# A short-convolution mixer on one core: u tiles that begin inside a 64-byte line of SBUF

## The chip, the core and the metric

The kernel runs on one NeuronCore of a Trainium2 chip. A core has a matrix engine (TensorE, PE in the profile; its weight loads are listed as PEld), three elementwise engines (VectorE or DVE, ScalarE or ACT, GpSimd or POOL) and a queue engine (SyncE or SP) that issues most transfers. They share SBUF, a memory of 128 partitions, and meet through semaphores. The time is microseconds on the device for one execution. Before: median 773.86 us of 3 runs (773.32 to 774.14).

## What is computed

One layer of an encoder trunk on x of 1024 frames by 1024 channels, fp32: a norm, four projections of 2048 channels each, a causal convolution of three taps, two gates, a projection back, a second norm and the residual.

```python
def short_conv_mixer(u, w_in, conv_w, w_out):
    z, bg, cg, v = jnp.split(u @ w_in.astype(u.dtype), 4, axis=-1)
    y = bg * causal_dwconv(cg * v, conv_w) * jax.nn.silu(z)
    return y @ w_out.astype(u.dtype)

u = rms_norm(h, pre_norm[i])
m = short_conv_mixer(u, sc_w_in[j], sc_conv_w[j], sc_w_out[j])
h = h + rms_norm(m, post_norm[i])
```

## The kernel before

**Products.** Every fp32 operand is split into a high part and a low part of type fp32r, and each product is three matmuls: low by high, high by low, high by high. The 2x2 block product of a projection is done with seven block products (a, b, c, d, e, f, g) instead of eight, after Strassen and Winograd, and three of these (b, f, g) are split into seven smaller ones once more for most column blocks. The operand of the moving side is a **u tile**, `u_a` to `u_g`: 2 parts x 4 k-blocks x 512 columns of fp32r, 16,384 bytes in each partition. The stationary side is a weight block of 128 x 128 out of a **page** of 2,048 bytes, which VectorE and ScalarE split as it comes in from HBM. So a block product is 12 matmuls of 512 columns, all reading one u tile; each writes one PSUM bank.

```python
nc.tensor.matmul(ps, lo, UH[i][:, k], start=first and k == 0, stop=False, skip_group_check=True)
nc.tensor.matmul(ps, hi, UL[i][:, k], start=False, stop=False, skip_group_check=True)
nc.tensor.matmul(ps, hi, UH[i][:, k], start=False, stop=last, skip_group_check=True)
```

The first argument after the bank is the stationary operand, the second the moving one. The profile names a matmul by bank, moving tile and stationary tile: `px<-u_d,wdh` moves `u_d` over the high part of weight block d.

**The smaller products** of b, f and g move 256 columns. Some of them move halves of `u_b`, `u_f` and `u_g`; the others move sums that were built once and are kept in tiles of their own, named `ubch_deep`, `ubgl_deep` and so on, in a pool (`tmp`) behind the pages.

**The stages.** A head (to about 40 us) loads x, norms and transposes it and builds the u tiles; then 32 pairs of weight columns (two for each of 16 channel blocks) run through the products, while VectorE adds results out of PSUM, runs the convolution and splits the next weights; from about 610 us the output projection runs, with both sides split into tiles of the same pool as the u tiles: `ou_a` to `ou_g` move, `oy_a` to `oy_g` are stationary; for the smaller products `oA..`, `oB..` and `ox..`. All of these are called u tiles here, since they are made with the tag `u`.

**Order.** The kernel is recorded first and then arranged by a planner (`Plan`), which simulates the engines with costs of its own and writes out one fixed order for each engine. It knows sizes and uses, not addresses.

**Memory.** In each partition SBUF holds, from the bottom: a scratch and small constants, the pool `up` with seven buffers for u tiles, 32 pages, and `tmp`. All buffers of `up` and all pages begin on a multiple of 64 bytes. The first tile of `tmp` is `gpad`, 1,026 floats, 4,104 bytes, which is rounded to 4,128; the `deep` tiles are stacked behind it and so begin 32 bytes into a 64-byte line.

**Lines.** The class `Tile` (from line 161) makes the real tile in `get`; every operation is issued from line 252, a helper, so the profile gives all of them as L252 and they are told apart by their tiles. The tiles with the tag `u` are made in `new_u` (line 802), for the second half of x (`xb`, line 989), in `third_unit` (1540), `split_pages` (1553) and `split_small` (1609).

Of the kernel before, what the change touches and what calls it, by code (L numbers as in the profile page):

```python
# [157 lines left out]
        return out  # L158


class Tile(View):

    __slots__ = ("pool", "args", "kw", "made", "parts", "writes", "reads", "left", "space", "key", "read", "summed", "n", "slot")
# [11 lines left out]
    def get(self):  # L175
        if self.made is None:
            kw = self.kw
            if kw["tag"] == "pg":
                kw = dict(kw, tag=f"pg{self.slot}", bufs=1)
            self.made = self.pool.pool.tile(list(self.args[0]), self.args[1], **kw)  # L180
        return self.made


# [1882 lines left out]
```

## Time and profile before

| | |
|---|---|
| median of 3 runs | 773.86 us (773.32 to 774.14) |
| the profiled execution | 772.83 us |
| its span, first to last instruction | 771.0 us |
| mean granted TensorE clock | 0.998 |
| HBM read, written | 101.74 MB, 44.30 MB |
| span, mean rate | 189 GB/s |

The busy time of an engine is what the profile calls busy: instructions in flight, without queue work. Matmuls overlap: one is issued while the one before it is still draining, so a group's mean (`390`) is the time that one takes from its own start to its own end, longer than the distance to the next one's start. In a row of the timeline the first figure is the start in us from the start of the span, the second the duration of the row's instructions together, and `x63` says that 63 of them were merged. A row of the waits reads: who waited, for whom, total us, times, longest.

### The profile page before, as it was taken

What the parts mean: (1) busy time and instruction counts of PE and PEld (TensorE: products, weight loads), DVE (VectorE), ACT (ScalarE), POOL (GpSimd) and SP (SyncE); (2) the same over time, 40 slices, a digit from 0 to 9 for tenths busy, and PEclk for the clock granted to TensorE, in tenths of its full rate; (3) what the DMA queues carried; (4) which work ended last, traced back from release to release, by engine and by line L of the source; (5) the groups of instructions that cost most, each with busy time, mean ns of one, the idle gap of its engine ahead of it and who ended that gap; (6) DMA issues with size and microseconds to landing.
All of it is one profiled execution on the core that took longest, in us unless ns stands there. A gap on an engine that the chain in (4) does not pass through costs nothing.

```text
span 771.0 us, 12816 instructions
## 1 busy us (share of the span) xinstructions
PE 762.2 (99%) x4320; PEld 669.6 (87%) x4320; DVE 673.9 (87%) x1022; ACT 458.8 (60%) x880; POOL 462.2 (60%) x416
## 2 busy tenths in 40 slices
PE   8999999999999999999999999999999999999996
PEld 7888889898889898888888898988888889889885
DVE  6899988989988978989999989798999898877993
ACT  7765678575656565556556565556653656564831
POOL 2519997889575778696789777584739100600321
PEclk9999999999999999999999999999999999999999
DMA  9222325243333547576858474927465998666842
GB/s 318 66 56 82 119 85 152 101 126 131 97 116 96 171 111 209 126 191 158 239 137 254 116 215 107 249 84 213 122 180 174 335 367 293 197 218 206 274 150 109
DMA packets 117137, 130.11 MB, mean 169 GB/s; under 512 B 7320, under 2 KB 74704, under 8 KB 116944
## 3 DMA queue, kind: packets, MB, share of 16 engines
q1 hardware_dynamic: 112560, 120.77, 49.0%
q0 software_dynamic: 4352, 8.39, 7.1%
q8 instruction: 34, 0.56, 0.3%
q14 instruction: 31, 0.25, 0.1%
q10 hardware_dynamic: 160, 0.14, 0.0%
HBM read 101.74 MB, written 44.30 MB: 189 GB/s over the span
## 4 chain that ended last, share of the span: by engine, by line
PE 98%; DVE 1%; DMA 0%; ACT 0%; POOL 0%; issue 0%; POOLq 0%; ACTq 0%
PE px L252 39%; PE pv L252 15%; PE po_x L252 11%; PE px2b L252 5%; PE px2f L252 4%; PE px2g L252 3%; PE po_v L252 3%; PE pp L252 3%; PE pv2b L252 3%; PE pv2f L252 2%; PE pf_x L252 1%; PE pb_x L252 1%; PE py2b L252 1%; PE pv2g L252 1%; PE py L252 1%; PE pf_v L252 1%
## 5 line engine op out<-in xcount | busy, mean ns | idle before, releaser
L252 PE MATMUL px<-u_d,wdh 128*128 128x512 f32 x248 | 76.8, 390 | 0.0
L252 PE MATMUL px<-u_a,wah 128*128 128x512 f32 x248 | 76.7, 390 | 0.0
L252 PE MATMUL pv<-u_e,weh 128*128 128x512 f32 x248 | 76.7, 390 | 0.0
L252 PE MATMUL px<-u_c,wch 128*128 128x512 f32 x248 | 76.6, 390 | 0.0
L252 ACT COPY beside<-raw 128x512 f32<-128x512 f32 x67 | 39.6, 591 | 31.8 <-DVE wal L252 11.0
L252 PEld LDWEIGHTS px<-u_d,wdh 128*128 128x128 f32 x248 | 46.6, 188 | 9.1
L252 PEld LDWEIGHTS px<-u_c,wch 128*128 128x128 f32 x248 | 46.7, 188 | 9.0
L252 PEld LDWEIGHTS px<-u_a,wah 128*128 128x128 f32 x248 | 46.7, 188 | 8.9
L252 PEld LDWEIGHTS pv<-u_e,weh 128*128 128x128 f32 x248 | 46.6, 188 | 8.9
L252 DVE SCALAR_TENSOR_TENSOR cv<-gpad,cw,cv 128x1024 f32<-128x1024 f32 x32 | 49.7, 1554 | 3.4 <-ACT cv L252 3.3
L252 POOL TENSOR_TENSOR sf<-raw,sc 128x512 f32<-128x512 f32 x30 | 44.5, 1482 | 10.9 <-DVE sc L252 6.0
L252 PE MATMUL px<-u_d,wdl 128*128 128x512 f32 x124 | 48.7, 393 | 0.0
L252 PE MATMUL px<-u_a,wal 128*128 128x512 f32 x124 | 48.7, 393 | 0.0
L252 PE MATMUL px<-u_c,wcl 128*128 128x512 f32 x124 | 48.5, 392 | 0.0
L252 PE MATMUL pv<-u_e,wel 128*128 128x512 f32 x124 | 48.5, 391 | 0.0
L252 POOL TENSOR_TENSOR sc<-se,raw 128x512 f32<-128x512 f32 x25 | 36.5, 1460 | 19.0 <-DVE se L252 10.0
L252 ACT COPY sna<-px 128x512 f32<-128x512 f32 x30 | 17.6, 586 | 49.4 <-PE px L252 47.7
L252 POOL TENSOR_TENSOR raw<-raw,raw 128x512 f32<-128x512 f32 x31 | 44.8, 1446 | 3.3 <-DVE se L252 1.9
L252 POOL TENSOR_TENSOR rs_post<-ve_post,minus_half 128x1 f32<-128x1 f32 x7 | 5.4, 784 | 68.1 <-DVE ve_post L252 68.1
L252 POOL TENSOR_TENSOR se<-raw,raw 128x512 f32<-128x512 f32 x22 | 33.1, 1504 | 17.7 <-DMA raw<-in_sc_w_in 5.7
L252 DVE TENSOR_TENSOR wcl<-sc,wch 128x512 fp32r<-128x512 f32 x31 | 31.6, 1020 | 2.6 <-ACT wch L252 2.6
L252 DVE TENSOR_TENSOR sna<-px2b,sna 128x256 f32<-128x256 f32 x56 | 23.2, 413 | 11.9 <-PE px2b L252 11.9
(486 smaller groups left out, 2637.1 us busy)
## 6 DMA issues: line engine op xcount, KB each, us to landing
raw<-in_sc_w_in SPq DMA_DIRECT2D x128, 256.0 KB, 4.6
y_d<-cv SPq DMA_DIRECT2D x16, 512.0 KB, 3.1
s_d<-s SPq DMA_DIRECT2D x32, 256.0 KB, 4.8
t_d<-in_sc_w_out POOLq DMA_DIRECT2D x16, 512.0 KB, 8.2
tb<-in_sc_w_out SPq DMA_DIRECT2D x16, 256.0 KB, 3.0
t_d<-in_sc_w_out SPq DMA_DIRECT2D x16, 256.0 KB, 4.5
t_d<-t_d SPq DMA_DIRECT2D x16, 256.0 KB, 4.5
s<-y_d SPq DMA_DIRECT2D x16, 256.0 KB, 4.7
```

The source lines that it names most:

```text
L252: getattr(engine, name)(*(self.plain(a) for a in args), **{k: self.plain(a) for k, a in kw.items()})
```

## The change

A u tile is asked for with 64 bytes more than it needs, as a flat row, and the tile that is used is a view of that row which begins some floats in: 8, 4, 12 or 2 floats, so 32, 16, 48 or 8 bytes. Which of them is taken from a table by the first letter of the last part of the tile's name: `u_a` and `ou_a1` have `a`, `oA1_b` and `ox_b` have `b`. `xb`, the second half of x, stays at 0. The planner's costs, the order on all engines and the waits are the same as before; so are the sizes of all operands. The buffers of `up` lie 16,448 instead of 16,384 bytes apart, and everything behind them begins 448 bytes later.

```diff
+EDGES = {"x": 0, "a": 8, "c": 4, "d": 12, "e": 2, "b": 4, "f": 8, "g": 12, "A": 4, "B": 8}
...
-            self.made = self.pool.pool.tile(list(self.args[0]), self.args[1], **kw)
+            shape = list(self.args[0])
+            if kw["tag"] == "u":
+                at, whole = EDGES[kw["name"].split("_")[-1][0]], int(np.prod(shape[1:]))
+                t = self.pool.pool.tile([shape[0], whole + 16], self.args[1], **kw)[:, at : at + whole]
+                names = "abcd"[: len(shape) - 1]
+                sizes = dict(zip(names[1:], shape[2:]))
+                self.made = t.rearrange(f"p ({' '.join(names)}) -> p {' '.join(names)}", **sizes)
+            else:
+                self.made = self.pool.pool.tile(shape, self.args[1], **kw)
         return self.made
```

| bytes into the line | tiles |
|---|---|
| 8 | `u_e`, `ou_e`, `oy_e` |
| 16 | `u_b`, `u_c`, `ou_c`, `oy_c`, `oA.._b`, `oB.._b`, `ox_b` |
| 32 | `u_a`, `u_f`, `ou_a`, `oy_a`, `oA.._f`, `oB.._f`, `ox_f` |
| 48 | `u_d`, `u_g`, `ou_d`, `oy_d`, `ou_g`, `oy_g` |

## The prediction

> **What bounds the kernel now.** I read the page first: which engine is full, and which the chain of waits runs through.
>
> ```profile
> span 771.0 us, 12816 instructions
> PE 762.2 (99%) x4320; PEld 669.6 (87%) x4320; DVE 673.9 (87%) x1022; ACT 458.8 (60%) x880; POOL 462.2 (60%) x416
> ...
> PE 98%; DVE 1%; DMA 0%; ACT 0%; POOL 0%; issue 0%; POOLq 0%; ACTq 0%
> ```
>
> PE holds 98% of the chain. A busy PE may still be a waiting PE, so the waits of PE alone came next:
>
> ```profile
> PE pw L252 <- DVE idle L252: 1.1, 1, 1.1
> PE pp L252 <- ACT u_a L252: 0.5, 1, 0.5
> PE pk L252 <- DVE xa L252: 0.3, 1, 0.3
> ```
>
> Three waits, 1.9 us, all on the way to the first products. From then on PE runs matmul after matmul, and the time is the number of matmuls times the distance between two starts. Only what changes that distance counts. The means in the groups (389 ns) are latencies of overlapping instructions and do not give it; the timeline does.
>
> ```profile
> L252 PE MATMUL po_x<-ou_g,oy_g 128*128 128x512 f32 x96 | 21.9, 389 | 0.0
> ...
> 749.81 14.44 PE L252 MATMUL po_x<-ou_g,oy_g 128*128 128x512 f32 x63
> ```
>
> 63 matmuls of 512 columns end 14.44 us after the first start, the last of them 0.389 us long: (14.44 - 0.39) / 62 = 226.6 ns from start to start. Now the 256-column ones, in one stretch where two kinds stand side by side:
>
> ```profile
> 127.29 0.28 PE L252 MATMUL px2b<-ubgh_deep,dwb 128*128 128x256 f32 x1
> ...
> 127.99 0.28 PE L252 MATMUL pv<-ufgh_deep,dwf 128*128 128x256 f32 x1
> ...
> 128.69 0.28 PE L252 MATMUL px<-u_g,dwg0l 128*128 128x256 f32 x1
> ...
> 129.41 0.28 PE L252 MATMUL px2g<-u_g,dwg0l 128*128 128x256 f32 x1
> ...
> 130.13 0.40 PE L252 MATMUL px<-u_a,wal 128*128 128x512 f32 x1
> ```
>
> Twelve matmuls that move a `deep` tile take 128.69 - 127.29 = 1.40 us, 116.7 ns each; twelve that move u_g take 130.13 - 128.69 = 1.44 us, 120.0 ns each. Same columns, same kind of weights, no wait in either. In the layout the u tiles begin on a 64-byte line and the `deep` tiles 32 bytes into one (they are stacked behind gpad, 4,104 bytes long). So the trace of before already holds the experiment, at one offset: 32 bytes are 3.3 ns faster than 0.
>
> From 512 to 256 columns the distance falls by 226.6 - 120.0 = 106.6 ns, 0.416 ns a column. What is left at 0 columns, 120.0 - 106.6 = 13.4 ns, is a fixed charge per matmul: 32 columns' worth at offset 0, and 24 columns' worth (10.1 ns) at offset 32. The 8 columns saved are 32 bytes of fp32: just what the first line no longer holds.
>
> **The change part by part.** No instruction is added, removed or moved on any engine, and the semaphores waited for are the same. What moves are addresses. (1) The moving operand of every matmul on a u tile starts 8, 16, 32 or 48 bytes into a line; so does the stationary one in the output products. (2) A u tile is 64 bytes longer, so u buffers spread by 64 bytes each and all pages behind shift by 448 bytes, whole lines. The `deep` tiles keep their 32 bytes.
>
> How many matmuls get which offset is counted from the groups; three of them for d and three for g, and three for e:
>
> ```profile
> L252 PE MATMUL px<-u_d,wdh 128*128 128x512 f32 x248 | 76.8, 390 | 0.0
> L252 PE MATMUL px<-u_d,wdl 128*128 128x512 f32 x124 | 48.7, 393 | 0.0
> L252 PE MATMUL po_x<-ou_d,oy_d 128*128 128x512 f32 x96 | 21.9, 389 | 0.0
> L252 PE MATMUL px<-u_g,wgh 128*128 128x512 f32 x56 | 17.3, 390 | 0.0
> L252 PE MATMUL px<-u_g,wgl 128*128 128x512 f32 x28 | 10.9, 390 | 0.0
> ...
> L252 PE MATMUL pv<-u_e,weh 128*128 128x512 f32 x248 | 76.7, 390 | 0.0
> L252 PE MATMUL pv<-u_e,wel 128*128 128x512 f32 x124 | 48.5, 391 | 0.0
> L252 PE MATMUL po_v<-ou_e,oy_e 128*128 128x512 f32 x96 | 21.9, 389 | 0.0
> ```
>
> With 512 columns: at 48 bytes d 248 + 124 + 96 and g 56 + 28 + 96 = 648; at 8 bytes e 468 and 24 in the first products = 492; at 32 bytes a 492 (as e) and f 84 = 576; at 16 bytes c 468 (as d) and b 60 = 528. With 256 columns: b 504 at 16, f 480 at 32, g 288 at 48. Together 3,516.
>
> Only 32 bytes have a price in the trace. For 8, 16 and 48 I bound it by the rows next to them. Floor: they change nothing, as at 0; then only 576 + 480 = 1,056 matmuls save 3.33 ns, 3.5 us. Ceiling: what counts is not the first line but the last, which 8 bytes of offset leave nearly empty; then the shortest offsets save most (5.8 ns at 8, 5.0 at 16, 3.3 at 32, 1.7 at 48, which is the same line read from the other end) and the sum is 2.9 + 5.2 + 3.5 + 1.6 = 13.1 us. Below nothing, too: see the slower rival. I take the straight line through the two points that are measured, 0.104 ns a byte, because it says what the 8 saved columns say: 0.83, 1.67, 3.33 and 5.00 ns. The sum: 492 x 0.83 = 0.4 us, 1,032 x 1.67 = 1.7, 1,056 x 3.33 = 3.5, 936 x 5.00 = 4.7; **10.3 us** of the 752 us in which PE runs products, 1.4%.
>
> Where would a faster PE meet a limit? First the head, where VectorE builds the u tiles just in time:
>
> ```profile
> 42.59 2.35 DVE L252 TENSOR_TENSOR u_c<-xb,u_c 128x1024 fp32r<-128x1024 f32 x2
> ...
> 48.34 2.35 DVE L252 TENSOR_TENSOR u_d<-xa,u_d 128x1024 fp32r<-128x1024 f32 x2
> ...
> 45.15 0.39 PE L252 MATMUL px<-u_c,wcl 128*128 128x512 f32 x1
> ...
> 50.59 0.39 PE L252 MATMUL px<-u_d,wdl 128*128 128x512 f32 x1
> ```
>
> u_c is done at 44.94 and used at 45.15; u_d is still being written when its first half is used. What PE gains before 50.6 us, 38 x 1.4% = 0.5 us, it waits away again. Then the middle and the DMA stretch:
>
> ```profile
> 550.00:600.00 50.00, 50.00 (x267) 43.23 (x266) 46.64 (x66) 24.73 (x45) 33.49 (x27) 1.00 0.57 175
> 600.00:650.00 50.00, 50.00 (x282) 43.98 (x282) 45.60 (x81) 29.08 (x53) 2.93 (x2) 1.00 0.95 328
> ```
>
> In its fullest late window VectorE (46.64, the third figure with a count) still idles 3.4 us of 50, five times the 0.7 us by which PE shortens it, so it keeps up. The DMA engines are 95% busy from 600 to 650 us (0.95, last but one); I count the 0.7 us of that stretch as lost. The closest handover in between:
>
> ```profile
> 419.01 0.68 DVE L252 TENSOR_TENSOR wdl<-beside,wdh 128x512 fp32r<-128x512 f32 x1
> ...
> 419.89 0.40 PE L252 MATMUL px<-u_d,wdl 128*128 128x512 f32 x1
> ...
> DVE sna L252 <- PE px2b L252: 11.9, 14, 1.6
> ```
>
> 0.20 us early. But VectorE has no lead of its own to lose: it waits for PE in turn (one such wait 14 times, about once in each of the 37 us rounds), so it moves forward with PE, and of the 6 us gained until then at most one round's 0.5 us can meet this margin. That is 0.3 us at the one or two tightest places; I charge nothing and leave it to the range. That VectorE and ScalarE now write u tiles off the line I cost at nothing: a `deep` tile, 32 bytes off, is written as fast as a page that stands on a line,
>
> ```profile
> 98.14 0.69 DVE L252 TENSOR_TENSOR dwf0l<-beside,dwf0h 128x512 fp32r<-128x512 f32 x1 [0.93 <-ACT beside L252]
> ...
> 99.68 0.69 DVE L252 TENSOR_TENSOR ubcl_deep<-beside,ubch_deep 128x512 fp32r<-128x512 f32 x1 [0.34 <-ACT beside L252]
> ```
>
> and there are some 300 such writes in 700 us.
>
> Gain: 10.3 - 0.5 - 0.7 = 9.1 us. The profiled execution took 772.83 us (its span of 771.0 and 1.8 around it), 1.0 under the median of 773.86. Against it the sum gives 763.7, against the median **764.8 us**.
>
> **Rivals.** *Only whole halves of a line help* (0.16): 32 and 48 bytes save 3.33 ns, 8 and 16 nothing: 1,056 + 936 = 1,992 matmuls, 6.6 us, less 0.9 in the two stretches: 768.2. For it: 32 is the only offset seen.
>
> *The last line decides* (0.10): the ceiling above, 13.1 - 1.2: 762.0. For it: the `deep` rows cannot tell first from last, since 32 bytes leave 8 columns in both.
>
> *The offset is not the cause* (0.07): the `deep` tiles also lie elsewhere in SBUF, behind the pages. Then 773.9, or a little more if a start inside a 16-byte piece makes one more piece to fetch: 4 columns at 0.416 ns, 1.7 ns on the 492 matmuls at 8 bytes, 0.8 us, 774.7. Against it: u tiles lie from 3 to 118 KB and all show 120.0 or 226.6. The Trainium skill's "SBUF — State Buffer", section "Specifications (TRN2)", speaks for this rival: it gives SBUF lines of 16 bytes with a penalty for each crossing to a new one, so that 16, 32 and 48 should be as good as 0 and 8 slightly worse. The rows above disagree: 32 bytes, two such lines on, read 116.7 ns against 120.0.
>
> *Slower* (0.13): a start that is not on 32 bytes costs one more half line per matmul, 8 columns, because the row of 512 or 256 columns then begins and ends in a piece of a half. That is 528 + 492 + 648 + 504 + 288 = 2,460 matmuls at 8, 16 and 48 bytes; at +3.33 ns each 8.2 us, against 3.5 us saved at 32 bytes: +4.7 us, 778.6. It decides from 3.5 / 2,460 = 1.4 ns a matmul. Against it, on another engine:
>
> ```profile
> L252 DVE SCALAR_TENSOR_TENSOR cv<-gpad,cw,cv x32: 1268/1334/2317, 67.8 to 612.0; 128x1024 f32<-128x1024 f32 x32
> ```
>
> half of these read gpad from byte 4 of a line and half from byte 8. VectorE's 512 columns above took 0.69 us, so 1,024 columns in 1,268 ns leave no room for anything read twice. For PE nothing shows it either way.
>
> Inside the forecast (0.54) there is a smaller fork: if the distance between moving and stationary operand counts, not the line, then the output products, where both move alike, gain nothing: 2.4 us of the 10.3, 767.2.
>
> **How the numbers follow.** Faster by over 0.2% (1.5 us, about what this kernel's measurement can tell from no change): forecast, halves, last line, 0.54 + 0.16 + 0.10 = 0.80. Within: 0.07. Slower: 0.13. The range runs from 760.5, below the last-line case by the spread of the runs, to 772.0, where only the 32-byte tiles pay (773.9 - 3.5 + 1.2 = 771.6); no change and slower, 0.20, stay out.
>
> **What would show it.** Blocks of twelve 512-column matmuls in the late timeline, start to start: 225.8 ns for e, 224.9 for c, 223.3 for a, 221.6 for d and g; 256-column blocks of b 118.3, f 116.7, g 115.0. All of PE's waits together should grow by no more than 1.2 us. If e is the quickest, the last line rules; if c and e stay at 226.6, the halves; if c, d and e rise above 226.6, the slower rival; if a and f do not fall, the offset was never the cause. The forecast is also wrong if the distances fall as said and the span does not: then a wait that PE did not have before takes it.

## The result

| | before | after |
|---|---|---|
| median of the runs | 773.86 us (773.32 to 774.21) | 780.96 us (780.76 to 781.33) |
| ratio of the medians | | 1.0093 (95% interval 1.008 to 1.0107) |
| the profiled execution | 772.83 us | 780.93 us |
| its span | 771.0 us | 779.2 us |
| mean granted TensorE clock | 0.998 | 0.998 |

The change makes the kernel slower by 0.93%, where 1.2% faster was predicted; the time lies outside the range. The first view of the page of the changed kernel, the engines' busy time and the shares of the chain:

```profile
span 779.2 us, 12816 instructions
...
PE 770.4 (99%) x4320; PEld 668.0 (86%) x4320; DVE 673.3 (86%) x1022; ACT 458.9 (59%) x880; POOL 462.1 (59%) x416
...
PE 98%; DVE 0%; DMA 0%; ACT 0%; POOL 0%; issue 0%; POOLq 0%; ACTq 0%
```

The span has grown by 8.2 us and PE's busy time by the same 8.2 us (762.2 to 770.4). No other engine has more to do: VectorE went from 673.9 to 673.3 us, ScalarE from 458.8 to 458.9. PE's waits in the changed kernel (who waited, for whom, total us, times, longest):

```profile
PE pw L263 <- DVE idle L263: 1.1, 1, 1.1
PE pp L263 <- ACT u_a L263: 0.5, 1, 0.5
PE pk L263 <- DVE xa L263: 0.4, 1, 0.4
```

They are the same three, 2.0 us instead of 1.9. So nothing waits longer, and the loss lies in the distance between the starts of two matmuls. First the stretch that the prediction read, in the timeline after the change (start, duration):

```profile
129.81 0.28 PE L263 MATMUL px2b<-ubgh_deep,dwb 128*128 128x256 f32 x1
...
131.21 0.28 PE L263 MATMUL px<-u_g,dwg0l 128*128 128x256 f32 x1
...
132.62 0.39 PE L263 MATMUL px<-u_a,wal 128*128 128x512 f32 x1
...
135.42 0.28 PE L263 MATMUL px<-u_g,dwg2l 128*128 128x256 f32 x1
```

Twelve matmuls that move a `deep` tile take 131.21 - 129.81 = 1.40 us as before. Twelve of 256 columns that move u_g take 1.41 us, 117.5 ns each, a gain of 2.5 ns (5.0 was predicted). The twelve of 512 columns behind them, on u_a, take 135.42 - 132.62 = 2.80 us, 233.3 ns each, where 223.3 was predicted. The same block of u_e, at the same place of the program, before the change:

```profile
102.27 0.39 PE L252 MATMUL pv<-u_e,wel 128*128 128x512 f32 x1
...
104.99 0.28 PE L252 MATMUL px2b<-u_b,dwb0l 128*128 128x256 f32 x1
```

and after it:

```profile
104.60 0.39 PE L263 MATMUL pv<-u_e,wel 128*128 128x512 f32 x1
...
107.39 0.28 PE L263 MATMUL px2b<-u_b,dwb0l 128*128 128x256 f32 x1
```

2.72 us became 2.79: 226.7 ns, then 232.5. And the output projection, in long unbroken rows, before:

```profile
720.54 21.95 PE L252 MATMUL po_x<-ou_d,oy_d 128*128 128x512 f32 x96
742.33 21.92 PE L252 MATMUL po_x<-ou_g,oy_g 128*128 128x512 f32 x96
```

and after:

```profile
689.81 18.39 PE L263 MATMUL po_v<-ou_e,oy_e 128*128 128x512 f32 x76
...
727.97 22.26 PE L263 MATMUL po_x<-ou_d,oy_d 128*128 128x512 f32 x96
750.07 22.40 PE L263 MATMUL po_x<-ou_g,oy_g 128*128 128x512 f32 x96
```

From the start of ou_d to that of ou_g, 96 matmuls, it was 21.79 us (227.0 ns) and is 22.10 (230.2). For ou_e, 8 bytes into its line, (18.39 - 0.40) / 75 = 239.9 ns, the longest of all.

Over the whole kernel, interval times count for every u and `deep` tile, from the starts of the records in the two traces: the 2,243 matmuls of 512 columns take 513.0 us before and 523.4 after, the 1,974 of 256 columns 234.5 and 231.9. The sum is +10.4 - 2.5 = +7.9 us of the span's 8.2. So the short matmuls gained, as predicted though by less, and the long ones lost instead of gaining.

### The profile page after: what moved, and what is told of

It reads as the page before. It is cut to its first block, busy times and chain, and to the rows that moved or that the text cites. A ratio compares the mean times of both kernels' runs of the same rounds, so it can differ in the third digit from the quotient of the medians.

```text
span 779.2 us, 12816 instructions
## 1 busy us (share of the span) xinstructions
PE 770.4 (99%) x4320; PEld 668.0 (86%) x4320; DVE 673.3 (86%) x1022; ACT 458.9 (59%) x880; POOL 462.1 (59%) x416
## 4 chain that ended last, share of the span: by engine, by line
PE 98%; DMA 0%; DVE 0%; ACT 0%; POOL 0%; issue 0%; POOLq 0%; ACTq 0%
PE px L263 39%; PE pv L263 15%; PE po_x L263 11%; PE px2b L263 5%; PE px2f L263 4%; PE px2g L263 3%; PE po_v L263 3%; PE pp L263 3%; PE pv2b L263 3%; PE pv2f L263 2%; PE pf_x L263 1%; PE pb_x L263 1%; PE py2b L263 1%; PE pv2g L263 1%; PE py L263 1%; PE pf_v L263 1%
```

## The experiments

The change does two things to addresses. It puts tiles into their lines, and by the 64 bytes that it adds to each buffer it spreads the seven buffers (buffer i moves by 64 i) and moves the pages by 448. **Distance** below is the start of the moving row less that of the stationary row, modulo 256 bytes, from the layout of each kernel. Before, it is 0 for every u tile, over the pages and in the output products, and 32 for the `deep` tiles. The expectations weigh two kinds of reading: that a tile's own start in its line counts (L, later O), and that it is where the two rows lie to each other (S, later R).

**1. The spread alone, and the edges in two halves.** The table of the change with other numbers; the 64 bytes stay.

```diff
-EDGES = {"x": 0, "a": 8, "c": 4, "d": 12, "e": 2, "b": 4, "f": 8, "g": 12, "A": 4, "B": 8}
+EDGES = {'x': 0, 'a': 0, 'c': 0, 'd': 0, 'e': 0, 'b': 0, 'f': 0, 'g': 0}
```

This is the first kernel. For the second, a, c, d and e keep their edges and b, f and g have 0; for the third it is the other way round.

> All u tiles begin on a line again (offset 0), but keep the 64 bytes that are added to each, so that buffers spread and pages shift as in the change. Theory L: weight loads and the moving stream of TensorE meet in SBUF, each meeting costs a step of some 6.7 ns, and how many there are depends on where in its line each begins; on the line, blocks of 512 columns settle at 226.7 ns. L expects 773.9 us (772.5 to 775.3) and 226.7 ns in the second half of a block. Rival S: the offset in the line does not matter, the new distances between buffers do: 781 us, as the change.

> Offsets only for the tiles a, c, d, e, which move 512 columns; b, f, g are at 0. From the traces of before and of the change the intervals of these tiles grew by 2.1 + 1.7 + 1.5 + 1.6 us (u_a, u_c, u_d, u_e) and by 0.6 + 0.0 + 0.3 + 1.2 us in the output products, 9.0 us in all. Theory L expects 782.9 us (781 to 785), above the change itself. Rival S: 781 us, as the change. Rival M (the 256-column blocks of b, f, g carry the loss by the way they hand over to the next block): 774 to 776.

> Offsets only for b, f, g; a, c, d, e are at 0. The 256-column matmuls gained 2.5 us in the change, the few 512-column ones of b, f and g lost 1.4 us. Theory L expects 772.8 us (771 to 775): 512-column blocks of a, c, d, e settle at 226.7 ns again, those of 256 columns stay near 117 to 119 ns. Rival S: 781. Rival M: 779 to 781.

Measured: 779.40 us, ratio 1.0072 (1.0056 to 1.0087); 781.98 us, 1.0105 (1.0089 to 1.012); 779.24 us, 1.0071 (1.0056 to 1.0086); the kernel before beside them 773.56 us. With every tile at the start of a line the kernel loses 5.8 us, most of the change's loss. u_e in the timeline of the first:

```profile
103.93 0.40 PE L263 MATMUL pv<-u_e,wel 128*128 128x512 f32 x1
...
106.73 0.28 PE L263 MATMUL px2b<-u_b,dwb0l 128*128 128x256 f32 x1
```

2.80 us, 233.3 ns, on a line. So the place in the line is not what made this block slow. The edges of the long ones cost 2.6 us more, those of the short ones nothing that shows (-0.2). The two don't simply add up: with both, the change itself (780.96) lies 1.0 us under the second kernel. In the first kernel the output products have several distances at once, and the interval goes with them: 227.4 ns at 0 (226.7 once settled), 229 at 64, 233 at 128 and at 192.

**2. The distance alone.** The kernel before, u tiles untouched; 32 bytes ahead of the pages and 32 behind them, so that pages start 32 bytes into a line and the `deep` tiles stay where they were in theirs. The distance of u tiles to the pages becomes 224; in the output products, where both rows are u tiles, it stays 0.

```diff
+    gap2 = ctx.enter_context(tc.tile_pool(name="gap2", bufs=1)).tile([P, 8], F32, tag="gap2", name="gap2")
     pages = plan.pool(ctx.enter_context(tc.tile_pool(name="pages", bufs=PAGES)), PAGES)
+    gap3 = ctx.enter_context(tc.tile_pool(name="gap3", bufs=1)).tile([P, 8], F32, tag="gap3", name="gap3")
```

> All u tiles on the line as before; instead all pages, that is the stationary operands, begin 32 bytes into a line, and the deep tiles keep their 32. Theory L, by which both starts count: the 512-column blocks no longer settle at 226.7 but run at 230 to 235 ns, about +10 us, less up to 3 us from 256-column blocks: 779 to 785 us. Rival O (only the moving operand's own start counts): 773.9 us, no change.

Measured: 779.52 us, 1.0073 (1.0056 to 1.009). Three rows of the tiles in the kernel before (fastest / median / slowest duration in ns, time of the first and last):

```profile
L252 PE MATMUL px<-u_c,wch x248: 389/389/398, 45.4 to 601.6; 128*128 128x512 f32 x124
...
L252 PE MATMUL po_v<-ou_e,oy_e x96: 389/389/389, 678.6 to 700.2; 128*128 128x512 f32 x96
...
L252 PE MATMUL px2b<-ubgh_deep,dwb x56: 277/279/283, 127.3 to 612.1; 128*128 128x256 f32 x56
```

and the same in this one:

```profile
L252 PE MATMUL px<-u_c,wch x248: 392/395/397, 46.3 to 608.1; 128*128 128x512 f32 x124
...
L252 PE MATMUL po_v<-ou_e,oy_e x96: 389/389/389, 685.3 to 706.8; 128*128 128x512 f32 x96
...
L252 PE MATMUL px2b<-ubgh_deep,dwb x56: 275/276/281, 130.1 to 618.7; 128*128 128x256 f32 x56
```

No u tile has moved. Those over the moved pages are slower; those over other u tiles run as before, `ou_e` at 389 without an exception in both (226.7 ns from start to start in both).

**3. Everything by 32 bytes.** One gap of the same 32 bytes ahead of the u tiles instead: u tiles and pages both start 32 bytes into a line, the `deep` tiles on one, and all distances are those of before.

```diff
+    gap1 = ctx.enter_context(tc.tile_pool(name="gap1", bufs=1)).tile([P, 8], F32, tag="gap1", name="gap1")
     up = plan.pool(ctx.enter_context(tc.tile_pool(name="up", bufs=7)), 7)
```

> One gap of 32 bytes ahead of the u tiles moves everything behind it alike: u tiles and pages now begin 32 bytes into a line, the deep tiles on a line, and the distance of every moving row to every stationary row is that of before. Theory R, formed from the first four runs (the distance between moving and stationary row, taken modulo 512 bytes or a part of it, decides; distance 0 settles at 226.7 ns): 773.6 us (772.5 to 775), u_d 229 ns, deep 117.4 ns. Rival O (the moving row's own place in its line decides, as the prediction had it): u tiles of 256 columns 116.7, deep 120, 512 columns away from 226.7: 765 if these save as predicted, 780 if they lose as in the change.

Measured: 773.25 us, 1.000 (0.9991 to 1.0009), and the rows of its tiles

```profile
L252 PE MATMUL px<-u_c,wch x248: 387/389/398, 45.9 to 602.2; 128*128 128x512 f32 x124
...
L252 PE MATMUL px2b<-ubgh_deep,dwb x56: 277/279/283, 127.8 to 612.7; 128*128 128x256 f32 x56
```

are those of before. The `deep` tiles keep their interval, 117.4 ns, although they now start on a line, and u_g keeps 119.3 although it now starts 32 bytes into one: the reading on which the prediction stood is refuted for the one offset that it had.

**4. The period.** A gap ahead of the pages of 256, 512 and 128 bytes (`[P, 64]`, `[P, 128]`, `[P, 32]` in the line of experiment 2, without the second gap). Every tile stays at the place in its line that it had.

> u tiles as before, pages and all behind 256 bytes later: distance 256. Output products, with both operands among the u tiles, keep distance 0 and 226.7 ns under any theory. Theory R with a period of 256 bytes (in the run with spread buffers, output blocks at distance 256 ran at 227.4 ns): 773.6 us (772.5 to 775.5). Theory R with a period of 512: 512-column blocks against pages at 230 to 235 ns, 779 to 783 us.

> u tiles as before, pages and all behind 512 bytes later. Theory R: nothing changes, 773.6 us (772.5 to 775), since the four weight blocks of a page already lie 512 bytes apart and all settle alike. Rival A (the absolute distance or the page's place in a larger unit decides, 1,024 bytes or more): 779 to 783 us.

> u tiles as before, pages and all behind 128 bytes later. If the period is 256 bytes and no less, 512-column blocks against pages run at about 232.5 ns as u_d did at distance 128 in the run with spread buffers, against 229 before: 1,764 blocks of them x 3.5 = +6 us, less 1 to 2 us from 256 columns: 777 to 781. If the period is 128: 773.4.

Measured: 773.55 us, 1.0002 (0.9993 to 1.0011); 773.34 us, 0.9999 (0.999 to 1.0008); 779.06 us, 1.0077 (1.0063 to 1.0091). u_c in the first of them:

```profile
L252 PE MATMUL px<-u_c,wch x248: 389/389/398, 45.5 to 602.0; 128*128 128x512 f32 x124
```

and with 128 bytes:

```profile
L252 PE MATMUL px<-u_c,wch x248: 390/393/404, 46.1 to 607.7; 128*128 128x512 f32 x124
```

256 more bytes change nothing and 128 cost as much as the whole spread. So distances count modulo 256 bytes, as far as these runs can tell.

**5. The `deep` tiles at 64.** The gap behind the pages alone: only the `deep` tiles move, from 32 bytes into a line to the start of the next, and from distance 32 to 64.

> Only the deep tiles move, by 32 bytes: they now begin on a line, at distance 64 to their weights instead of 32. Theory R: 115.9 ns per matmul instead of 117.4, as in the run with pages at 32, 702 of them: 1.0 us less, 772.6. Rival O, the prediction's reading of the deep rows: on the line 120.0 ns, 1.8 to 2.3 us more, 775.4 to 775.9.

Measured: 774.14 us, 1.0012 (1.0004 to 1.0021). Both readings missed. The `deep` tiles went from 117.4 to 118.2 ns,

```profile
L252 PE MATMUL px2b<-ubgh_deep,dwb x56: 279/281/283, 127.5 to 613.4; 128*128 128x256 f32 x56
```

where experiment 2, at the same distance, had 115.9. Two things differ between the two: there the `deep` tiles lay 32 bytes into their line, and their neighbours had other distances. u_g, which has not moved, went from 119.3 to 119.9, so blocks of 256 columns also depend on what runs around them. The run doesn't say which of the two it was. The trace of experiment 2 shows that the place in the line isn't needed for such a difference: with every `deep` tile 32 bytes into its line and at distance 64, those with names in `ubg`, `ubd`, `ufg` and `ufd` run at 113 to 114 ns there in most of their blocks, those with names in `ubc`, `ufc`, `ugc`, `ugd` and `ugg` at 117 to 119 in most of theirs.

**6. The spread, with the distances put back.** The spread of the change with 128 bytes instead of 64, so that pages move by 896, and each u tile placed 0 or 128 bytes into its buffer by a table of names, such that every distance is 0 again.

```diff
-                at, whole = EDGES[kw["name"].split("_")[-1][0]], int(np.prod(shape[1:]))
-                t = self.pool.pool.tile([shape[0], whole + 16], self.args[1], **kw)[:, at : at + whole]
+                at, whole = EDGES[kw["name"]], int(np.prod(shape[1:]))
+                t = self.pool.pool.tile([shape[0], whole + 32], self.args[1], **kw)[:, at : at + whole]
```

> Buffers of u spread by 128 bytes each (twice the change's step) and pages shifted by 896 bytes, but each u tile is placed in its buffer so that its distance to every stationary row is a multiple of 256 bytes again. Theory R with the period of 256: 773.4 us (772.5 to 774.5), 226.7 ns settled. Rival S (spreading the buffers costs by itself, whatever the distance): 779 to 781.

Measured: 773.29 us, 1.000 (0.9991 to 1.0009), and u_c is back:

```profile
L263 PE MATMUL px<-u_c,wch x248: 389/389/398, 45.9 to 602.4; 128*128 128x512 f32 x124
```

Larger buffers and moved pages cost nothing once the distances are right.

**7. Using it.** As 6, in two kernels. In the first, the moving sums of the small output products (`oB..`, 256 columns) stand at other distances from their stationary ones: 192 bytes, one of them 64. In the second, u_b and u_g stand at 192 and u_f at 64 as well, which touches both their 256-column matmuls and the 512-column ones that read the same tiles. Some entries of the table, in floats, first those that both kernels change, then those that only the second does:

```diff
-... 'oB1_b': 0, 'oB3_b': 0, 'oA1_b': 32, ...
+... 'oB1_b': 16, 'oB3_b': 16, 'oA1_b': 0, ...
...
-... 'u_b': 32, ... 'u_f': 0, ... 'u_g': 32, ...
+... 'u_b': 16, ... 'u_f': 16, ... 'u_g': 16, ...
```

> Placement as in the restored one, but the moving tiles of the smaller output products stand 192 bytes from their stationary ones (one of them 64). In the change and in the spread run such long 256-column blocks ran at 113.3 to 117.8 ns instead of 120.0. 240 at 192 bytes x (120 - 115.7) and 48 at 64 bytes x 2.2: 1.1 us less, 772.2 (771.5 to 773).

> As the one with the output tiles, and u_b, u_f and u_g too stand 192, 64 and 192 bytes from their weights; a, c, d, e keep distance 0. Theory R by the intervals of the spread run: 936 matmuls of 256 columns x (119.4 - 117.2) = 2.1 us less, 228 of 512 columns x 4.5 = 1.0 us more, output 1.1 us less: 771.2 us. What could spoil it: blocks of 512 columns that follow an unsettled 256-column block may take longer to settle; each matmul more costs up to 9 ns, some 95 blocks: then 772 to 774.

Measured: 772.53 us, 0.9989 (0.998 to 0.9998); 772.26 us, 0.9991 (0.9982 to 1.0), against 773.32 for the kernel before beside them. One of the products, before:

```profile
L252 PE MATMUL pb_y<-oB_b,oA_b x24: 283/283/283, 639.6 to 642.3; 128*128 128x256 f32 x24
```

and in the first kernel of this experiment:

```profile
L263 PE MATMUL pb_y<-oB_b,oA_b x24: 276/277/293, 639.7 to 642.3; 128*128 128x256 f32 x24
```

The short ones do gain, and the first kernel is 0.1% faster than the one before. The second, whose runs lie between 772.00 and 773.28, can't be told from the first: the gain on u tiles is eaten by the long matmuls. Against the first kernel its trace has 2.0 us less on 256 columns (233.6 to 231.6) and 2.8 us more on 512 (513.0 to 515.8), 0.7 us of which are four matmuls near 558 and 561 us with intervals of 307 to 510 ns. 512 columns on u_g went from 227.6 to 233.2 ns without the three of these four that are on u_g (240.7 with them), on u_b from 232.2 to 238.0, and u_a, which has not moved but follows u_g in the stretch shown above, from 230.9 to 232.3. Its row of u_g, with one of the late ones as the slowest:

```profile
L263 PE MATMUL px<-u_g,wgh x56: 388/394/497, 57.1 to 615.9; 128*128 128x512 f32 x56
```

The mean intervals side by side, in ns from start to start, worked out from the starts of the records in each trace (in brackets the distance):

| columns, tile | before | the change | spread alone | pages +32 | all +32 | pages +128 | put back |
|---|---|---|---|---|---|---|---|
| 512, u_a | 230.9 (0) | 236.2 (160) | 234.5 (128) | 235.2 (224) | 231.0 (0) | 235.3 (128) | 231.0 (0) |
| 512, u_c | 228.4 (0) | 232.9 (208) | 232.4 (192) | 233.1 (224) | 228.7 (0) | 232.0 (128) | 228.4 (0) |
| 512, u_d | 229.0 (0) | 233.1 (176) | 232.5 (128) | 233.2 (224) | 229.0 (0) | 232.8 (128) | 229.4 (0) |
| 512, u_e | 228.8 (0) | 232.9 (200) | 233.9 (192) | 233.2 (224) | 228.9 (0) | 233.4 (128) | 228.8 (0) |
| 256, u_b | 119.2 (0) | 118.7 (80) | 116.8 (64) | 118.8 (224) | 119.2 (0) | 118.2 (128) | 119.2 (0) |
| 256, u_f | 119.5 (0) | 117.1 (32) | 118.9 (0) | 118.4 (224) | 119.5 (0) | 118.2 (128) | 119.6 (0) |
| 256, u_g | 119.3 (0) | 118.0 (112) | 116.9 (64) | 118.3 (224) | 119.3 (0) | 118.3 (128) | 119.3 (0) |
| 256, `deep` | 117.4 (32) | 116.9 (32) | 117.4 (32) | 115.9 (64) | 117.4 (32) | 116.9 (32) | 117.6 (32) |

The row of u_a includes the 24 first products in the head, which are slow in every run; without them it reads 228.9 before, 234.4 in the change and 232.6 in the spread. In the column of the spread u_f stands at 118.9 between two at 116.8 and 116.9: it is the one whose buffer moved by 192 bytes, the pages' 448 modulo 256, and so kept its distance.

At 512 columns u_f went from 226.9 to 230.3 in that kernel all the same, although its distance is 0. Its five blocks behind u_d, which stands at 128, settle anew: the intervals run 234, 231, 233, 236, 224, 231, 236, 228, 232, 230, 227, 227 ns. Before the change, with u_d at 0 ahead of it, the same block ran at 226.7 from its first matmul.

## Why the prediction was wrong

**What bounds the kernel** was read rightly. PE carries 98% of the chain before and after, its waits grew by 0.1 us, and interval times count gives 7.9 of the 8.2 us. Writing u tiles off the line cost nothing, as said, and VectorE kept up.

**The step that failed** is the reading of one pair of rows. The prediction took the 3.3 ns between a `deep` tile and u_g as "a fixed charge per matmul, 32 columns' worth at offset 0, and 24 columns' worth at offset 32" - "just what the first line no longer holds". The two kinds of block differed in two things: in the place in the line (32 against 0) and in the distance to the stationary row (32 against 0). Experiment 3 changes the first and not the second: no change. Experiment 2 changes the second and not the first for the u tiles: +6.0 us; the gap of 128 bytes leaves every tile's place in its line as it was and changes only the distance: +5.7. The number of columns fitted both, and the trace of before could not part them.

**The price was then carried from 256 columns to 512.** Of the sum of 10.3 us, 3.9 stood on matmuls of 256 columns and 6.4 on those of 512, by its own counts and prices. No row of before shows a 512-column matmul at any distance but 0. The first part measured 2.5, of the right sign (2.2 of it on the u tiles, the rest on the `deep` tiles, which the sum left out); the second measured a loss of 10.4. The same shift that shortens 256 columns by up to 2.4 ns (u_f) lengthens 512 columns by 4 to 5 (u_a, c, d, e in the table). The sign was read from the wrong shape.

**"Whole lines".** The prediction noted that buffers spread by 64 bytes and pages move by 448, and costed it at nothing because it was whole lines. By experiment 1 this was the largest cost of the change: 5.8 us, against 7.1 for the whole change. The edges add the rest; between the two traces the 512-column matmuls took 1.7 us more and the 256-column ones the same.

**The rivals.** The *offset is not the cause* (0.07) was right about the cause but expected no change. The *slower* rival (0.13) named a time 2.4 us under the measured one by a mechanism that fell: a charge at 8, 16 and 48 bytes. u_a, at 32, lost too, and with all tiles on a line the loss is there. The fork "if the distance between moving and stationary operand counts, not the line" named the right variable and gave it 767.2 us, because it took the sign from the same pair of rows, and because it let both rows of an output product move alike, though they lie in buffers that the spread moves by different steps (0 to 192 bytes apart after the change). *Halves* and *last line* expected the long matmuls to gain, and fell with the forecast. Of the signs, c, d and e rose, which stood for the slower rival, and a and f did not fall at 512 columns, which stood for the offset not being the cause; experiments 1 and 3 decide for the second, for the largest part of the loss.

**What was shown and what was not.** That the distance decides, modulo 256 bytes, is shown for the spread, and so for most of the loss, by the gaps of 32, 128, 256 and 512 bytes and by putting the distances back. That the two streams that PE reads, the moving rows and the next weights, get in each other's way in SBUF is argued from it: the rows of the weight loads don't show it, their median is 188 ns before and after. The place in the line is not without effect either. In the output products both rows carry the same edge, so that the change and the spread alone have the same distances there: at 32 bytes nothing differs (ou_a 233.2 and 232.8), at 16 it is faster (ou_c 229.2 to 227.0 ns), at 48 slower at a distance of 0 (ou_d 227.4 to 230.2) and slightly faster at 128 and 192 (ou_g 232.7 to 231.6), and at 8 much slower (ou_e 231.2 to 239.6). Why these differ stays open, and with them the 1.3 us or so of the change that the spread doesn't explain. Edges of 8, 16 or 48 bytes over pages at a distance of 0 were not tried.

## What to carry to other kernels

Padding or shifting an SBUF tile changes where it lies to every tile that is read beside it; here the start of the moving row less that of the stationary row, modulo 256 bytes, was worth 3.5 to 5 ns of about 229 in the mean 512-column matmul over pages (u_a, c, d, e at a distance of 32 to 128 bytes either way), so a spread by "harmless" multiples of 64 bytes cost 0.7%. Before a price is read from two rows of a profile, list everything in which they differ, addresses to each other included, and don't carry it to another shape: here the sign turned between 256 and 512 columns. Where PE never waits, time blocks of equal matmuls from start to start; the means of the groups (390 ns for u_c before, 395 after) are durations that overlap, not the distance, and say nothing of the cause.

## What the hardware showed

- A stream of 512-column matmuls, each with its own weights, settles at 226.7 ns from start to start at a distance of 0 modulo 256 bytes; at others the blocks ran mostly at 229 to 240. One of 256 columns settles at 120.0, and at others ran mostly at 113.6 to 119. In these runs the two sizes want opposite things.
- The Trainium skill, "TensorE: Matmul & The Clock Gate", section "Step-by-step: what each phase is for", gives PE two independent SBUF read ports, so that loading the next weights takes no read bandwidth from the running matmul. The measured intervals are hard to square with that: in experiment 2 u_c stayed where it was and only the pages and what lies behind them moved, and it went from 228.4 to 233.1 ns. Whether the ports, the memory or something else is the cause, no run shows.
- An interval settles slowly: before the change a block of 512 columns that follows one of 256 needs five to seven matmuls (234, 236, 228, 232, 231 ns in one case) until it stands at 226.7; behind another of 512 at distance 0 it runs at 226.7 from its first matmul. So u_a, behind a short block in the stretch shown, has a mean of 229.0 in such blocks before, and a block's interval can depend on its neighbour's distance, as for u_f in the spread and u_a in experiment 7. At other distances a block need not end at one value: at 192, in the spread, u_c ends at 236 and 231 ns in turn, and u_e behind u_f at 233.
